# An encoder layer in a list-scheduled kernel: later copies, another DRAM layout, fixed engines for low parts, longer score runs, and a list that may hold an engine back

## The chip, the cores and the metric

The kernel runs on one NeuronCore of a Trainium2 chip. The metric is the device time of one execution in microseconds; the kernel before is given as the median of three runs. One further execution was taken with the hardware profiler.

## The reference

One encoder layer with shared weights is applied to two batches: a prompt of 512 tokens and a sample of 1024 tokens, both 1024 wide.

```python
h = rmsnorm(x, norm_g)
proj = h @ w_in
qa, ka, va, za, qb, kb, vb, zb, ga, gb = jnp.split(proj, ...)
qa = rmsnorm(qa..., qn_a)
ka = rmsnorm(ka..., kn_a)
oa = neighbourhood_attention(qa, ka, va, rpb_a) * jax.nn.silu(za)
oa = oa @ w_o_a
qb = rmsnorm(qb..., qn_b)
kb = rmsnorm(kb..., kn_b)
ob = window_gqa_attention(qb, kb, vb, t5_table, sink_b) * jax.nn.silu(zb)
ob = ob @ w_o_b
merged = jax.nn.sigmoid(ga) * oa + jax.nn.sigmoid(gb) * ob
return x + merged @ w_out
```

Branch A has 8 heads of 64; each query sees a clamped window of 8 rows by 16 columns on a grid 64 wide, with a bias per head (`rpb_a`). Branch B has 8 query heads on 2 key heads, a band of 128 tokens to either side, a T5 bias and a sink logit.

## The kernel before

Products are made in fp32r with both factors split into a high and a low part, three matmuls for each product: high by high, low by high, high by low. For activations the parts are `hh` and `hl`, for weights `whi` and `wlo`. A low part is one subtraction, source less high part.

The program has four stages one after the other: attention of the prompt (0 to about 220 us), its dense part (to about 394), attention of the sample (394 to about 787), its dense part (to the end). TensorE takes products of a next stage as filler (written to PSUM tag `d`) while it works on attention.

**Attention** goes through six groups: four of branch A (two heads each) and two of branch B (four heads each). A group's weights are loaded and split (L603, L605, L610), its token tiles are projected (L764, tag `p`), squared and summed (`sq` L783, `ss` L788), GpSimd makes the inverse norm (`rs_v` L795, `rs_r` L802), VectorE scales (`qk` L819), TensorE transposes (L864) into `kt` and `q`. Scores are products of 64-row halves of the array, two heads at once (L937), reduced with the bias and the maximum by VectorE (L972), exponentiated, transposed (L1029), weighed with v (L1066), and the tile `ot` is stored to DRAM `o_d` (L1090 for A, L1102 for B). The bias tables of a group are made from a mask and a loaded `raw` by L698. Branch B's projection reads copies `hb` of `hh` and `hl` in another token order (L665 on ScalarE, L667 on VectorE).

**The dense part** loads `ot` back (L1535, in `post_z`), multiplies by the SiLU of the product with z's weights, and stores `u_d` (L1520). Products in this part are of Strassen's form: their moving side are sums `T` of token blocks, stored beforehand in DRAM (`t_d`), loaded by L1245 and split into high and low in `split` (high on ScalarE L1172, low on VectorE or GpSimd L1177); the weights' sums `S` are split in the same way. The matmuls are at L1293 to L1295.

**What sets the order.** Every operation is entered in a class `Flow` with a list of (engine, time in ns) choices, its inputs, and a priority (smaller is more urgent). `Flow.run` plays the program through with these times: each engine that is free takes the most urgent ready operation that has room for its results; between two engines it takes the one that would be done first. Two-input operations of VectorE and GpSimd are kept apart in this plan. The order found becomes the fixed order of each engine's instructions; DMAs are issued in order by SP. On the chip each engine waits in this order for its semaphores. PSUM has banks of tag `p` (2), `x` (5, scores, transposes and sums share them) and `d` (1).

The steps of the prediction touch `project`, `attend`, `weigh`, `split`, `stored_sums`, `weight_tiles`, `post_z` and `Flow.run`.

Of the kernel before, what the change touches and what calls it, by code (L numbers as in the profile page):

```python
# [26 lines left out]
SLACK = 1.1  # L27
SCRATCH = 1024
# [12 lines left out]
P = 128  # L41
# [95 lines left out]
class Op:  # L137
    __slots__ = ("choice", "emit", "new", "vals", "after", "outs", "prio", "left", "lag", "key", "eng", "port")


class Flow:
# [20 lines left out]
    def op(self, choice, emit, prio, new=(), use=(), into=(), after=(), hold=(), lag=0, port=None):  # L162
# [6 lines left out]
        o.key, o.outs, o.eng = len(self.ops), [], None  # L169
# [37 lines left out]
    def run(self):  # L207
        import heapq

        for o in self.ops:  # L210
            o.left = len(o.after)
            for a in o.after:
                a.outs.append(o)
# [45 lines left out]

        def backlog(e, item):  # L260
            return max(free_at[e], now) + sum(dict(x.choice)[e] for p, k, x in ready[e] if (p, k) < item[:2] and x.eng is None)
# [5 lines left out]
        while done < len(self.ops):  # L267
            for e in ready:
                while free_at[e] <= now:
                    skipped, got = [], None  # L270
                    while ready[e]:
                        item = heapq.heappop(ready[e])
                        o = item[2]
                        if o.eng is not None:
                            continue
                        ns = dict(o.choice)[e]
                        if all(room(v, n) for v, n in o.new) and not any(locked(v, e) or v.held and not v.t for v in o.vals) and not barred(o, e) and all(
                            e2 == e or backlog(e2, item) + n2 >= now + ns - BIAS.get((e, e2), 0) for e2, n2 in o.choice
                        ):
# [18 lines left out]
                    if got.lag:  # L298
                        dma_free = max(dma_free, now + ns + 650) + got.lag
                        at(dma_free + 950, 2, got)  # L300
            if not events:
# [53 lines left out]
def encoder_kernel(  # L355
# [48 lines left out]
    o_d = {geo.nt: dpool.tile([2, 8, P, geo.nt], F32, tag=f"o_d{geo.nt}", name=f"o_d{geo.nt}") for geo in (gp, gs)}  # L404
# [246 lines left out]
    def attention_phase(geo, hh, hl, h_ops, mask_d, early, late):  # L651
# [79 lines left out]
        def project(br, w, t, prio):  # L731
# [10 lines left out]
            else:  # L742
# [6 lines left out]
                for q in range(2):  # L749
                    for m, v in enumerate((hh, hl)):  # L750
# [5 lines left out]
                            prio - 1, new=[hb[m][q]], hold=[v], after=[o for u in h_ops.values() for o in u], port=True,  # L756
# [154 lines left out]
        def attend(br, gi, g, batch, nb_t, info, prio):  # L911

            nh = 2 if br == "A" else 4
            k0 = 2 * (gi % 2)
            states = []
            for block in batch:
                sums = tuple(tile_([P, 4], F32, tag, 3) for tag in ("mx", "sm", "rs", "es"))
                pss = [bank("x") for _ in range(nh)]
# [7 lines left out]
            def emit(e):  # L926

                for block, _, pss, _ in states:
                    runs, tiles, width, step, whole = places(block)
                    q = queries(block)  # L930
                    for pair in range(nh // 2):
                        at = runs[0][0] if whole else pair * P
                        for n, (u, k) in enumerate(((0, 0), (0, 1), (1, 0))):
                            for i in range(2):
                                rows = slice(64 * i, 64 * i + 64)
                                kv = kt.t[rows, k0 + k].rearrange("p (t n) -> p t n", n=P)
                                pe.matmul(  # L937
                                    pss[2 * pair + i].t[:, :width], q.t[rows, u, at : at + P],
# [3 lines left out]
            def queries(block):  # L942
# [5 lines left out]
                (("pe", ns),), emit, prio, new=[v for _, _, pss, sbs in states for v in (*pss, *sbs)],  # L948
# [12 lines left out]
        def weigh(br, gi, g, block, sums, pss, sbs, nb_t, info, prio):  # L961
# [7 lines left out]
            def score(i, ps, sb):  # L969
                def emit(e, i=i, ps=ps, sb=sb):  # L970
                    init = 3.0e38 if br == "A" else nsink[:, 4 * g + i : 4 * g + i + 1]
                    dve.tensor_tensor_reduce(  # L972
                        out=sb.t[:, :width], in0=ps.t[:, :width], in1=bias_of(br, nb_t, i, table), scale=1.0,
# [18 lines left out]
            for i, (ps, sb) in enumerate(zip(pss, sbs)):  # L992
                score(i, ps, sb)
# [57 lines left out]
            for i in range(2):  # L1051
                for c in range(nw):
# [16 lines left out]
                    o = f.op((("pe", PE_(256 if br == "A" else 512)),), emit, prio, use=[v, pp], **kw)  # L1069
            ot = tile_([P, 4, P], F32, "ot_", 2)  # L1070
# [5 lines left out]
            if br == "A":  # L1076
# [10 lines left out]
                def emit():  # L1087
                    if len(runs) == 1:
                        dst = over(o_d[nt][0, g], runs).rearrange("(i p) n -> p i n", i=2)
                        nc.sync.dma_start(dst, ot.t[:64, ::2])  # L1090
                        return
                    for i in range(2):
                        dst = over(o_d[nt][0, g, 64 * i : 64 * i + 64], runs)
# [3 lines left out]
            else:  # L1097
                for e in range(2):
                    dst = o_d[nt][e, 4 + 2 * g : 6 + 2 * g, :, runs[0][0] : runs[0][0] + P]
                    dst = dst.rearrange("c (i d) n -> d (c i) n", d=64)  # L1100
                    o = sp(
                        lambda e=e, dst=dst: nc.sync.dma_start(dst, ot.t[e * 64 : e * 64 + 64]),  # L1102
                        131072, prio, use=[ot],
                    )
                    for c in (4 + 2 * g, 5 + 2 * g):
                        for n in range(nt // 512):
                            stores[c, n].append(o)
# [3 lines left out]
        for gi, (br, g) in enumerate(groups):  # L1111
# [14 lines left out]
            for t in range(nb):  # L1126
# [4 lines left out]
                size = 2 if br == "A" else 1  # L1131
# [7 lines left out]
    def dense_phase(geo, hh, hl, h_ops, o_stores, exps_done, start, opened, tp, up, p0, p1, p2, x_t, y_t, classic, fill, after_gates=None, side=None):  # L1139
# [28 lines left out]
        def split(hi, lo, src, n, prio, new_hi, new_lo, src_v, after=()):  # L1168
# [7 lines left out]
                any_tt(n),  # L1176
# [59 lines left out]
        def stored_sums(prio, d, after):  # L1236

            tv, ops = {}, {}
            for j in (1, 2, 0, 3):
                tv[j] = tuple(f.value(tp, [P, 4, nh], F32R, "T", 8) for _ in range(2))  # L1240
                vh, vl = tv[j]
                for k in range(4):
# [7 lines left out]
                        (vh, k == 0), (vl, k == 0), [st],  # L1250
# [9 lines left out]
        def weight_tiles(operands, per, prio):  # L1260
# [5 lines left out]
            for i, src in enumerate(operands):  # L1266
                at, q = [], 0
                while q < 4:
# [7 lines left out]
                        (hi, ti not in seen), (lo, ti not in seen), [src],  # L1276
# [72 lines left out]
        def pair_strassen(srcs, post, prio, mov_h, mov_t, seed=None, last=False, kept=None):  # L1349
# [11 lines left out]
            w = weight_tiles([*first, s2, s3, s1, raw[1, 1], s4], 6, prio - 0.5)  # L1361
# [162 lines left out]
        def post_z(c, a, n, v, in_psum, prio):  # L1524
# [3 lines left out]
            for e, ot in enumerate(ots):  # L1528
                if c < 4:
                    src, dst = o_d[nt][e, c, :, a : a + n], lambda ot=ot: ot.t[:, :n]  # L1530
                else:
                    src = o_d[nt][e, c].rearrange("p (i n) -> p i n", n=P)[:, :, a // nb : a // nb + m]
                    dst = lambda ot=ot: ot.t[:, :n].rearrange("p (i n) -> p i n", n=m)
                dma(
                    lambda dst=dst, src=src: nc.sync.dma_start(dst(), src), 512 * n, prio - 0.5, new=[ot],  # L1535
# [418 lines left out]
```

## Time and profile before

| | |
|---|---|
| median of 3 runs | 1136.02 us (1134.59 to 1136.24) |
| profiled execution | 1135.29 us, of it 1133.5 us span |
| granted TensorE clock | 1.00 |
| DMA issued by the kernel | 184.91 MB in 139010 packets |

The profile lists for each engine its busy time in the span and its share. A table by windows gives busy time by stretch. In a row of a timeline stand start, duration, engine, line, operation, output and input, count; in square brackets the idle time of the engine just before it and what ended that. The chain of waits is followed back from the last instruction. PE is TensorE, DVE VectorE, ACT ScalarE, POOL GpSimd, SPq the queue of SyncE.

### The profile page before, as it was taken

The page shows a single profiled execution, that of the slowest core. Times are in us where ns is not written, and L with a number is a line of the kernel's source. Part 1 is how long each engine was busy: PE and PEld are TensorE (multiplying, and loading weights), DVE is VectorE, ACT ScalarE, POOL GpSimd, SP SyncE. Part 2 cuts the span into 40 slices and gives each one's busy share as a digit, 9 for nine tenths or more (in the row PEclk, how much of TensorE's full clock was granted, in tenths as well). Part 3 has the DMA queues.
Part 4 walks back from the last instruction along what each step waited for, and adds up shares of the span by engine and source line. Part 5 has one row for each costly group of instructions (what it writes and reads, how often), then busy time and mean ns, then how long its engine had stood idle before and what let it go on. Part 6 is the DMA issues. An engine that isn't in the chain of part 4 may idle for free.

```text
span 1133.5 us, 18690 instructions
## 1 busy us (share of the span) xinstructions
PE 1119.0 (99%) x6079; PEld 973.2 (86%) x6079; DVE 860.1 (76%) x1988; ACT 651.9 (58%) x1499; POOL 337.3 (30%) x438
## 2 busy tenths in 40 slices
PE   8999999999999999999999999999999999999998
PEld 6999988888888889999999988988788888888887
DVE  5888797587776568787878888885988766677764
ACT  6777987644432257565769888876543335423430
POOL 4653433000011154434324344420333322222211
PEclk9999999999999999999999999999999999999999
DMA  7854543488886732121212314244977645867862
GB/s 263 276 155 138 184 115 103 110 257 248 256 278 216 254 128 91 27 63 30 82 41 85 81 38 112 57 131 121 307 241 234 224 156 170 281 207 222 280 215 93
DMA packets 139108, 186.11 MB, mean 164 GB/s; under 512 B 29897, under 2 KB 68561, under 8 KB 139010
## 3 DMA queue, kind: packets, MB, share of 16 engines
q1 hardware_dynamic: 139010, 184.91, 51.8%
q8 instruction: 48, 0.79, 0.3%
q14 instruction: 50, 0.41, 0.1%
HBM read 137.66 MB, written 51.92 MB: 167 GB/s over the span
## 4 chain that ended last, share of the span: by engine, by line
PE 93%; DMA 2%; DVE 2%; issue 1%; ACT 1%; POOL 1%; SPq 0%; DVEq 0%; ACTq 0%
PE p L764 25%; PE x L1294 9%; PE x L1295 9%; PE x L1293 9%; PE x L1066 5%; PE x L937 5%; PE x L1029 5%; PE d L1293 4%; PE d L1295 4%; PE d L1294 4%; PE p L1294 4%; PE p L1295 4%; PE p L1293 4%; PE x L864 2%; DMA w<-in_w_att_dram 1%
## 5 line engine op out<-in xcount | busy, mean ns | idle before, releaser
L764 PE MATMUL p<-whi,hh 128*128 128x384 f32 x384 | 133.4, 348 | 0.0
L764 PE MATMUL p<-whi,hl 128*128 128x384 f32 x384 | 132.2, 344 | 0.0
L764 PE MATMUL p<-wlo,hh 128*128 128x384 f32 x384 | 131.8, 343 | 0.0
L1172 ACT ACTIVATE whi<-raw 128x512 fp32r<-128x512 f32 (+1 forms) x140 | 81.4, 600 | 71.2 <-PE x L1294 22.3
L981 ACT ACTIVATE sb<-sb,mx 128x384 f32<-128x384 f32 (+1 forms) x192 | 107.8, 565 | 16.9 <-DVE mx L972 16.5
L1295 PE MATMUL x<-T,wlo 128*128 128x512 f32 x280 | 108.9, 389 | 0.0
L1294 PE MATMUL x<-T,whi 128*128 128x512 f32 x280 | 108.9, 389 | 0.0
L1293 PE MATMUL x<-T,whi 128*128 128x512 f32 x280 | 108.9, 389 | 0.0
L764 PE MATMUL p<-whi,hb 128*128 128x384 f32 x384 | 107.6, 346 | 0.0
L1177 POOL TENSOR_TENSOR wlo<-raw,whi 128x512 fp32r<-128x512 f32 (+1 forms) x33 | 39.5, 1204 | 215.6 <-DMA raw<-in_w_g_dram 112.9
L1040 DVE TENSOR_TENSOR pp<-x,pp 128x512 fp32r<-128x512 f32 (+1 forms) x136 | 82.5, 638 | 19.6 <-ACT pp L1035 19.0
L1177 DVE TENSOR_TENSOR wlo<-raw,whi 128x512 fp32r<-128x512 f32 (+1 forms) x107 | 72.0, 682 | 32.3 <-ACT whi L1172 28.7
L802 POOL TENSOR_TENSOR rs_r<-rs_v,mhalf 128x4 f32<-128x4 f32 (+1 forms) x72 | 80.5, 1118 | 5.7
L1035 ACT ACTIVATE pp<-x 128x512 fp32r<-128x512 f32 (+1 forms) x136 | 70.8, 559 | 15.8 <-PE x L1029 14.3
L1294 PE MATMUL x<-hl,whi 128*128 128x512 f32 x200 | 77.8, 389 | 0.0
L1295 PE MATMUL x<-hh,wlo 128*128 128x512 f32 x200 | 77.8, 389 | 0.0
L1293 PE MATMUL x<-hh,whi 128*128 128x512 f32 x200 | 77.8, 389 | 0.0
L1066 PE MATMUL x<-pp,v 128*128 128x256 f32 (+1 forms) x368 | 75.8, 322 | 0.0
L764 PEld LDWEIGHTS p<-whi,hl 128*128 128x128 f32 x384 | 72.6, 189 | 1.3 <-issue 1.0
L764 PEld LDWEIGHTS p<-wlo,hh 128*128 128x128 f32 x384 | 72.7, 189 | 1.0 <-issue 0.7
L764 PEld LDWEIGHTS p<-whi,hh 128*128 128x128 f32 x384 | 72.7, 189 | 0.7 <-DVE v L812 0.3
L764 PEld LDWEIGHTS p<-whi,hb 128*128 128x128 f32 x384 | 69.1, 188 | 3.1 <-issue 1.3
(388 smaller groups left out, 2965.1 us busy)
## 6 DMA issues: line engine op xcount, KB each, us to landing
raw<-in_w_g_dram SPq DMA_DIRECT2D x84, 256.0 KB
w<-in_w_att_dram SPq DMA_DIRECT2D x46, 384.0 KB
raw<-in_w_z_dram SPq DMA_DIRECT2D x40, 256.0 KB
ot<-o_d SPq DMA_DIRECT2D x36, 256.0 KB
g_d<-C SPq DMA_DIRECT2D x34, 256.0 KB
fr<-in_w_g_dram SPq DMA_DIRECT2D x28, 256.0 KB
raw<-in_w_out_dram SPq DMA_DIRECT2D x28, 256.0 KB
out_dram<-C SPq DMA_DIRECT2D x19, 256.0 KB
```

The lines of the kernel that those rows point to most:

```text
L764: pe.matmul(ps.t[:, :GW], part[u](k), mv.t[:, c], start=k == 0 and m == 0, stop=k == KC - 1 and m == 2,)
L802: lambda e: nc.gpsimd.tensor_tensor(r.t[:, :nn], rv.t[:, :nn], mhalf[:, :nn], op=ALU.pow),
L937: pe.matmul(pss[2 * pair + i].t[:, :width], q.t[rows, u, at : at + P], kv[:, tiles[0] : tiles[-1] + 1 : step], start=n == 0, stop=n == 2,)
L981: act.activation(sb.t[:, :width], sb.t[:, :width], AF.Exp, bias=mx.t[:, i : i + 1], scale=-1.0, accum_out=sm.t[:, i : i + 1],)
L1035: lambda e, pt=pt, pp=pp, nn=nn: act.activation(pp.t[:, 0, :nn], pt.t[:, :nn], AF.Copy),
L1040: lambda e, pt=pt, pp=pp, nn=nn: dve.tensor_tensor(pp.t[:, 1, :nn], pt.t[:, :nn], pp.t[:, 0, :nn].bitcast(F32), op=ALU.subtract),
L1066: pe.matmul(out(), v.t[:, vs], mv(), start=first, stop=last)
L1172: (("act", ACT_(n)),), lambda e: act.activation(hi(), src(), AF.Copy), prio,
L1177: lambda e: engines[e].tensor_tensor(lo(), src(), hi().bitcast(F32), op=ALU.subtract), prio,
L1293: pe.matmul(out, hi.t[:, cs], mh(), start=first and k == 0, stop=False, **more)
L1294: pe.matmul(out, hi.t[:, cs], ml(), start=False, stop=False, **more)
L1295: pe.matmul(out, lo.t[:, cs], mh(), start=False, stop=last and k == len(ws) - 1, **more)
```

## The change

There are five parts.

1. The copies `hb` wait, beside the normalised input, for the start of a step that lies six priorities ahead of them.
2. Branch B's attention output has a DRAM tensor of its own, `ob_d`, with 512 tokens in a row. A block of the prompt is stored in one DMA (128x4x128), a block of the sample in two (128x4x64, pieces of 256 bytes; before 64x4x128 in two, pieces of 512 bytes). Loads of it read whole rows of 2 KB; before, those of the sample read 8x64 (pieces of 256 bytes).
3. The low parts of the stored sums `T` from `t_d`, and of the weights of the first Strassen pair, go to VectorE alone.
4. The prompt's branch A scores of four blocks are one run of 24 matmuls instead of two runs of 12, and two blocks share a PSUM bank, in halves of 256 columns. The third and later kept z products wait for the last weighted sum of attention.
5. In attention, the list passes over an operation of ScalarE, VectorE or GpSimd if one that is more urgent by over 3 becomes ready within half of its duration.

The diff, cut to its core (line numbers of the kernel after are some 27 to 31 higher than before):

```diff
+PATIENT = ("act", "dve", "pool")
+URGENT = 3
+SHARE = 0.5
+DENSE_TOO = 0
+AHEAD = 6
...
+        def expect(o, end):
+            for x in o.outs:
+                x.open -= 1
+                x.eta = max(x.eta, end + min(self.LAG.get((o.eng, e), 100) for e, _ in x.choice))
+                if not x.open and x.eta > now:
+                    coming[x.choice[0][0]].append(x)
+
+        def sooner(o, e, ns):
+
+            if e not in PATIENT or o.slack == 1 and not DENSE_TOO:
+                return False
+            coming[e] = [x for x in coming[e] if x.eta > now and x.eng is None]
+            t = [x.eta for x in coming[e] if x.prio < o.prio - URGENT and x.eta < now + SHARE * ns]
+            if t:
+                at(min(t), 4, None)
+            return bool(t)
...
-... and not barred(o, e) and all(
+... and not barred(o, e) and not sooner(o, e, ns) and all(
...
-    o_d = {geo.nt: dpool.tile([2, 8, P, geo.nt], F32, ...) for geo in (gp, gs)}
+    o_d = {geo.nt: dpool.tile([4, P, geo.nt], F32, ...) for geo in (gp, gs)}
+    ob_d = {geo.nt: dpool.tile([geo.nt // 512, 8, P, 512], F32, ...) for geo in (gp, gs)}
...
-                            prio - 1, new=[hb[m][q]], hold=[v], after=[o for u in h_ops.values() for o in u], port=True,
+                            prio - 1, new=[hb[m][q]], hold=[v], port=True,
+                            after=[*(o for u in h_ops.values() for o in u), f.begun[nt, prio - AHEAD]],
...
+            shared = br == "A" and nt == NT_P
...
-                pss = [bank("x") for _ in range(nh)]
+                second = shared and len(states) % 2
+                pss = [(v, 256) for v, _ in states[-1][2]] if second else [(bank("x"), 0) for _ in range(nh)]
...
+            f.weighed = o
...
-                for e in range(2):
-                    dst = o_d[nt][e, 4 + 2 * g : 6 + 2 * g, :, runs[0][0] : runs[0][0] + P]
...
+                m, t = 512 // nb, runs[0][0] // P
+                for n in range(nt // 512):
+                    dst = ob_d[nt][n, 4 * g : 4 * g + 4, :, t * m : t * m + m].rearrange("a p m -> p a m")
...
-                size = 2 if br == "A" else 1
+                size = 1 if br == "B" else 4 if nt == NT_P else 2
...
-        def split(hi, lo, src, n, prio, new_hi, new_lo, src_v, after=()):
+        def split(hi, lo, src, n, prio, new_hi, new_lo, src_v, after=(), both=True):
...
-                any_tt(n),
+                any_tt(n)[: 1 + both],
...
-                        (vh, k == 0), (vl, k == 0), [st],
+                        (vh, k == 0), (vl, k == 0), [st], both=d is m_d,
...
-            w = weight_tiles([*first, s2, s3, s1, raw[1, 1], s4], 6, prio - 0.5)
+            w = weight_tiles([*first, s2, s3, s1, raw[1, 1], s4], 6, prio - 0.5, prio > 0)
...
-                    src = o_d[nt][e, c].rearrange("p (i n) -> p i n", n=P)[:, :, a // nb : a // nb + m]
+                    src = ob_d[nt][a // nh, 2 * c - 8 : 2 * c - 6, e * 64 : e * 64 + 64, :n]
...
-            o = product(ps, ws[0], mov_h(0, 0), i / 4 - 1, True, True)
+            o = product(ps, ws[0], mov_h(0, 0), i / 4 - 1, True, True, [f.weighed] if i > 1 else [])
```

TensorE issues the same matmuls before and after; VectorE has 26 rows of its order fewer and GpSimd 17 more, most of it bias tables and softmax scalings (`sb`) that change engines. The order of all engines is the same from about 825 us on. Three places show how the order moves.

The first is the start of the sample's attention, VectorE. `w_` with a number is a weight buffer of group 0 or 1. Before:

```order
L1177 TENSOR_TENSOR fl<-fr,fh 128x512
L610 TENSOR_TENSOR wlo<-w_4898,whi 128x768
L788 TENSOR_REDUCE ss<-sq 128x4
L812 TENSOR_TENSOR v<-p,v 128x2x64
L667 CAST hb<-hl 128x512 x2
L788 TENSOR_REDUCE ss<-sq 128x4
L819 TENSOR_TENSOR qk<-p,rs_r 128x256
```

After:

```order
L1207 TENSOR_TENSOR fl<-fr,fh 128x512 x2
L816 TENSOR_REDUCE ss<-sq 128x4
L840 TENSOR_TENSOR v<-p,v 128x2x64
L847 TENSOR_TENSOR qk<-p,rs_r 128x256
L637 TENSOR_TENSOR wlo<-w_4883,whi 128x768
```

The first `qk` follows its `ss` and `v` directly; the copies are gone from there, and a weight's low part comes behind. On GpSimd, before:

```order
L1166 TENSOR_TENSOR raw<-raw 128x512 x4
L1177 TENSOR_TENSOR fl<-fr,fh 128x512
L795 TENSOR_SCALAR rs_v<-ss 128x4
L802 TENSOR_TENSOR rs_r<-rs_v,mhalf 128x4
L795 TENSOR_SCALAR rs_v<-ss 128x4
```

After:

```order
L1196 TENSOR_TENSOR raw<-raw 128x512 x3
L823 TENSOR_SCALAR rs_v<-ss 128x4
L830 TENSOR_TENSOR rs_r<-rs_v,mhalf 128x4
L637 TENSOR_TENSOR wlo<-w_4891,whi 128x768
L725 TENSOR_TENSOR bias<-mask,raw 128x24x8
```

The first `rs_v` no longer stands behind a low part `fl`. On SP, where the loads for this place are issued, before:

```order
L1329 DMA s_d<-raw 128x512
L603 DMA w_4838<-in_w_att_dram 128x768
L1329 DMA s_d<-raw 128x512
L603 DMA w_4852<-in_w_att_dram 128x768
L1583 DMA out_dram<-C 128x512
L1329 DMA s_d<-raw 128x512 x2
L603 DMA w_4882<-in_w_att_dram 128x768
```

After:

```order
L1359 DMA s_d<-raw 128x512 x4
L1612 DMA out_dram<-C 128x512
L630 DMA w_4838<-in_w_att_dram 128x768
L630 DMA w_4846<-in_w_att_dram 128x768
L1633 DMA fr<-in_w_g_dram 128x512 x2
L1612 DMA out_dram<-C 128x512
L630 DMA w_4883<-in_w_att_dram 128x768
```

Group 0's weights move behind all of the `s_d` stores.

The second place is the second group of the sample's attention, VectorE, where its bias tables are made. Before:

```order
L812 TENSOR_TENSOR v<-p,v 128x2x64
L1083 TENSOR_TENSOR ot__5863<-ot__5863 64x2x128
L698 TENSOR_TENSOR bias<-mask,raw 128x24x8 x2
L698 TENSOR_TENSOR bias<-mask,raw 128x16x8 x2
L819 TENSOR_TENSOR qk<-p,rs_r 128x256
```

After:

```order
L1115 TENSOR_TENSOR ot__5801<-ot__5801 64x2x128
L847 TENSOR_TENSOR qk<-p,rs_r 128x256
L725 TENSOR_TENSOR bias<-mask,raw 128x24x8
L816 TENSOR_REDUCE ss<-sq 128x4
L725 TENSOR_TENSOR bias<-mask,raw 128x16x8
```

Two of the four table instructions leave VectorE there, and the other two stand behind a `qk` instead of ahead of it.

The third is the sample's z products, VectorE (`T` low parts, `S` sums, `C` and `ot` of the z gates). Before:

```order
L1177 TENSOR_TENSOR wlo<-S,whi 128x256
L1166 TENSOR_TENSOR U<-fr,x 128x512
L1177 TENSOR_TENSOR T<-U,T 128x512
L1166 TENSOR_TENSOR ot<-ot 128x512
L1177 TENSOR_TENSOR T<-w_10666,T 128x512
L1166 TENSOR_TENSOR C<-C,ot 128x512
L1166 TENSOR_TENSOR U<-U,x 128x512
```

After:

```order
L1207 TENSOR_TENSOR T<-fh,T 128x512
L1207 TENSOR_TENSOR T<-U,T 128x512
L1207 TENSOR_TENSOR T<-w_10643,T 128x512
L1207 TENSOR_TENSOR T<-U,T 128x512
L1196 TENSOR_TENSOR U<-U,x 128x512
L1196 TENSOR_TENSOR ot<-ot 128x512
```

The third set's `T` from `w_` stands ahead of the second `ot`, where it stood behind it.

More of the change, by code (lines that the diff above doesn't have):

```diff
@@ L137 @@
 class Op:
-    __slots__ = ("choice", "emit", "new", "vals", "after", "outs", "prio", "left", "lag", "key", "eng", "port")
+    __slots__ = ("choice", "emit", "new", "vals", "after", "outs", "prio", "left", "lag", "key", "eng", "port", "slack", "open", "eta")
 class Flow:
@@ L210, in run @@
         for o in self.ops:
-            o.left = len(o.after)
+            o.left = o.open = len(o.after)
+            o.eta = 0
             for a in o.after:
@@ L276, in run @@
                         ns = dict(o.choice)[e]
-                        if all(room(v, n) for v, n in o.new) and not any(locked(v, e) or v.held and not v.t for v in o.vals) and not barred(o, e) and all(
+                        if all(room(v, n) for v, n in o.new) and not any(locked(v, e) or v.held and not v.t for v in o.vals) and not barred(o, e) and not sooner(o, e, ns) and all(
                             e2 == e or backlog(e2, item) + n2 >= now + ns - BIAS.get((e, e2), 0) for e2, n2 in o.choice
@@ L403, in encoder_kernel @@
     t_d = dpool.tile([4, 4, P, NT_S // 2], F32, tag="t_d", name="t_d")
-    o_d = {geo.nt: dpool.tile([2, 8, P, geo.nt], F32, tag=f"o_d{geo.nt}", name=f"o_d{geo.nt}") for geo in (gp, gs)}
+    o_d = {geo.nt: dpool.tile([4, P, geo.nt], F32, tag=f"o_d{geo.nt}", name=f"o_d{geo.nt}") for geo in (gp, gs)}
+    ob_d = {geo.nt: dpool.tile([geo.nt // 512, 8, P, 512], F32, tag=f"ob_d{geo.nt}", name=f"ob_d{geo.nt}") for geo in (gp, gs)}
     s_d = dpool.tile([4, 4, P, 512], F32, tag="s_d", name="s_d")
@@ L947, in attend @@
             o = f.op(
-                (("pe", ns),), emit, prio, new=[v for _, _, pss, sbs in states for v in (*pss, *sbs)],
+                (("pe", ns),), emit, prio, new=[v for _, _, pss, sbs in states for v in (*(ps for ps, a in pss if not a), *sbs)],
                 use=[queries(block) for block in batch], after=[o for b in batch for t in b[1] for o in info[t][2]],
@@ L990, in score @@
                 x.vals = [*x.vals, mx]
-            for i, (ps, sb) in enumerate(zip(pss, sbs)):
-                score(i, ps, sb)
+            for i, ((ps, a), sb) in enumerate(zip(pss, sbs)):
+                score(i, ps, a, sb)
             if br == "B":
@@ L1088, in emit @@
                     if len(runs) == 1:
-                        dst = over(o_d[nt][0, g], runs).rearrange("(i p) n -> p i n", i=2)
+                        dst = over(o_d[nt][g], runs).rearrange("(i p) n -> p i n", i=2)
                         nc.sync.dma_start(dst, ot.t[:64, ::2])
@@ L1092, in emit @@
                     for i in range(2):
-                        dst = over(o_d[nt][0, g, 64 * i : 64 * i + 64], runs)
+                        dst = over(o_d[nt][g, 64 * i : 64 * i + 64], runs)
                         nc.sync.dma_start(dst, ot.t[:64, 2 * i].rearrange("p (a b) -> p a b", b=64))
```

29 lines of the change are left out of this document (14 added, 15 removed).

## The prediction

> **What bounds the kernel now.** I read the busy times first, then TensorE by stretches, then the waits of TensorE.
>
> ```profile
> span 1133.5 us, 18690 instructions
> PE 1119.0 (99%) x6079; PEld 973.2 (86%) x6079; DVE 860.1 (76%) x1988; ACT 651.9 (58%) x1499; POOL 337.3 (30%) x438
> ...
> 0.00:50.00 50.00, 44.03 (x249) 39.14 (x250) 34.90 (x94) 33.99 (x72) 24.23 (x40) 1.00 0.80 278
> 50.00:100.00 50.00, 50.00 (x325) 46.92 (x324) 40.29 (x129) 36.51 (x97) 29.49 (x48) 1.00 0.56 175
> ...
> 400.00:450.00 50.00, 48.16 (x308) 44.98 (x308) 38.57 (x114) 31.12 (x80) 24.63 (x34) 1.00 0.34 108
> 450.00:500.00 50.00, 49.24 (x334) 46.59 (x331) 40.94 (x119) 29.12 (x81) 18.24 (x29) 1.00 0.17 46
> 650.00:700.00 50.00, 49.77 (x317) 44.20 (x316) 44.14 (x121) 43.46 (x109) 20.05 (x30) 1.00 0.30 80
> ...
> 800.00:850.00 50.00, 47.52 (x206) 38.07 (x205) 46.19 (x67) 22.98 (x46) 18.43 (x13) 1.00 0.83 268
> ```
>
> The columns are the stretch, its length, then busy time of TensorE, weight loads, VectorE, ScalarE and GpSimd, the granted clock and the DMA share. TensorE works 99% of the span at a clock of 1.00, with 6079 matmuls that the change leaves as they are. So no change of copies or layouts can win much: what can be won is the holes in TensorE's row, and there are few. They lie at the start (5.97 us up to 50) and in the four other stretches below 50.00.
>
> ```profile
> PE x L1811 <- DMA rb<-in_norm_row_dram: 4.4, 1, 4.4
> PE x L864 <- DVE qk L819: 3.1, 3, 1.8
> PE d L1294 <- DVE T L1177: 1.6, 1, 1.6
> ...
> PE p L1294 <- DVE T L1177: 0.9, 2, 0.7
> ```
>
> Of the start, 4.4 is the first load, which the change does not touch. The rest are transposes that wait for a normalised q/k tile, and low-part products that wait for a low part T made by VectorE. I go through these places in turn, and measure a hole as the distance between two starts less the distance without a wait.
>
> **Place A, start of the sample's attention.**
>
> ```profile
> 403.98 0.40 PE L1294 MATMUL d<-hl,fh 128*128 128x512 f32 x1
> 404.21 0.40 PE L1295 MATMUL d<-hh,fl 128*128 128x512 f32 x1
> 406.45 0.44 PE L864 MATMUL x<-ident,qk 128*128 128x128 f32 x2 [1.84 <-DVE qk L819]
> ...
> 402.62 2.15 DVE L667 CAST hb<-hl 128x512 fp32r<-128x512 f32 x2
> 405.97 0.42 DVE L819 TENSOR_TENSOR qk<-p,rs_r 128x256 f32<-128x256 f32 x1 [0.75 <-POOL rs_r L802]
> ...
> 402.23 1.31 POOL L1177 TENSOR_TENSOR fl<-fr,fh 128x512 fp32r<-128x512 f32 x1 [11.40 <-ACT fh L1172]
> 403.62 1.22 POOL L795 TENSOR_SCALAR rs_v<-ss 128x4 f32<-128x4 f32 x1
> 404.92 1.01 POOL L802 TENSOR_TENSOR rs_r<-rs_v,mhalf 128x4 f32<-128x4 f32 x1
> ```
>
> Starts lie 2.24 apart; such a product takes 0.23 (404.21 less 403.98), so the hole is 2.0, some 0.17 more than the marked wait. The awaited qk needs rs_r, which GpSimd began late behind fl (1.31). The two casts of hb (2.15) sit on the same engine as qk and feed branch B, which comes some 200 us later. The change ties those copies to the start of a step near them, and in the new order fl is no longer ahead of rs_v, and VectorE takes qk before the next weight's low part. I take the whole 2.0 as gone. What is late next is the weights:
>
> ```profile
> 396.26 3.98 DMA w<-in_w_att_dram
> ```
>
> SP issued group 0's first two weights between the s_d stores; now all four s_d stores and an output store go ahead of the first weight, and two fr loads ahead of the third. A load of them took 3.98 to land (a row of the chain), so a shift of 2 to 3 us in the queue arrives as such, and the TensorE work between covers part of it. I put a new hole at 0.9, between 0 and 2.0 (the old one again). Net for A: −1.1, from −2.0 to 0.
>
> **Place B.**
>
> ```profile
> 465.02 1.57 DVE L698 TENSOR_TENSOR bias<-mask,raw 128x192 f32<-128x192 f32 x4 [0.65 <-DMA raw<-rpb_x]
> 466.52 0.41 DVE L819 TENSOR_TENSOR qk<-p,rs_r 128x256 f32<-128x256 f32 x1
> ...
> 465.97 0.34 PE L764 MATMUL p<-wlo,hh 128*128 128x384 f32 x1
> 467.08 0.30 PE L864 MATMUL x<-ident,qk 128*128 128x128 f32 x1 [0.76 <-DVE qk L819]
> ```
>
> Four bias tables waited 0.65 for a DMA, and qk stood behind them in VectorE's order: the hole is 1.11 − 0.17 = 0.94. After, GpSimd takes 16 of VectorE's bias instructions over the whole kernel, and the raw load is issued earlier; VectorE keeps two tables here. −0.8, from −0.94 to 0. The 0.23 missing between 650 and 700 I halve, with its start-to-start loss near 0.5 as the upper end: −0.3.
>
> **Place D, the sample's z products.**
>
> ```profile
> 785.75 1.24 SPq L1102 DMA_DIRECT2D o_d<-ot__10494  x2
> ...
> 791.71 2.14 SPq L1535 DMA_DIRECT2D ot<-o_d  x2
> ...
> L1520 SPq DMA_DIRECT2D u_d<-C x10: 319/428/3656, 791.3 to 838.1; - x10
> ...
> 803.77 6.24 DMA ot<-o_d
> ...
> 803.26 0.68 DVE L1177 TENSOR_TENSOR T<-U,T 128x512 fp32r<-128x512 f32 x1
> 810.10 1.25 DVE L1166 TENSOR_TENSOR ot<-ot 128x512 f32<-128x512 f32 x1 [0.46 <-DMA ot<-o_d]
> 811.27 1.75 DVE L1177 TENSOR_TENSOR T<-w,T 128x512 fp32r<-128x512 f32 x1
> ...
> 810.76 1.71 POOL L1177 TENSOR_TENSOR wlo<-raw,whi 128x512 fp32r<-128x512 f32 x1
> ...
> 811.11 0.40 PE L1293 MATMUL d<-T,whi 128*128 128x512 f32 x1
> 813.08 0.50 PE L1294 MATMUL d<-T,whi 128*128 128x512 f32 x1 [1.57 <-DVE T L1177]
> ...
> 818.37 0.50 PE L1294 MATMUL p<-T,whi 128*128 128x512 f32 x1 [0.24 <-DVE T L1177]
> ...
> 820.67 0.50 PE L1294 MATMUL p<-T,whi 128*128 128x512 f32 x1 [0.65 <-DVE T L1177]
> ```
>
> Two causes add up. The loads of ot from o_d come in 256-byte pieces: their issues take SP 2.14 for two, and the u_d store behind them took up to 3.66 to issue where the median of its line is 0.43, so t_d loads that stand behind go out some 3 us late, and ot itself landed after 6.24 (a row of the chain). VectorE waited for ot with T<-w behind it in order. And T took 1.75 beside a GpSimd instruction of 1.71, where the same T takes 0.68 alone. The holes: 1.97 − 0.23 = 1.74 at 813.08, again 0.17 above the marked wait; 0.24 and 0.65 become 0.41 and 0.82 in the same way, together 2.97. I allow 0.5 more for small ones around. The change makes branch B's loads contiguous 2 KB rows, issues the t_d loads ahead of them, keeps T on VectorE alone and lists it ahead of ot; GpSimd has no T in that stretch. VectorE carries one more T (0.68), in a stretch where it is 46.19 of 50 busy. −2.9, from −3.4 to 0.
>
> On the 256-byte pieces the change also does the reverse: 32 stores of the sample's branch B go from 512-byte to 256-byte pieces (the prompt's stay at 512). They lie in the sample's attention, where the DMA share was 0.17 and 0.30 in the stretches shown, and the first load from there was issued 4.7 us after the last store (791.71, and 785.75 with 1.24 of issue). I price them at 0; without that cover a store as slow as the 6.24 above would hold the first ot back by about 1.5 (6.24 − 4.7). The Trainium skill (DMA: Bandwidth & Descriptors, Specifications) says that transfers under 512 B fall to read-modify-write and miss the line rate; the trace's slow 256-byte loads agree, and by that rule these stores would be slower too, which is the third rival below.
>
> **Score runs.** Four prompt blocks now share one run, so four runs of TensorE's row-split mode fewer.
>
> ```profile
> 38.20 0.33 PE L764 MATMUL p<-wlo,hh 128*128 128x384 f32 x1
> 38.46 0.97 PE L937 MATMUL x<-kt,qt 64*128 64x256 f32 x12
> 39.37 0.44 PE L864 MATMUL x<-ident,qk 128*128 128x128 f32 x2
> ```
>
> Entering took 0.26 instead of 0.17, and the twelve took 0.91, where six pairs of 256 columns at half of 0.23 would be 0.69: 0.3 a run, four times 0.3 is −1.2, from −1.2 to 0. Against it: a run holds its four score banks of five until eight score reductions are done, not four. VectorE, 40.29 of 50 busy there, has room, and TensorE has projection and filler work to go on with, so I take no hole from it beyond the general one below. The prompt's hb copies leave the first stretch, whose holes beside the first load are 5.97 − 4.4 = 1.6, and its first tiles are moved: a quarter of that, −0.4, from −1.0 to +0.7. The z products that now wait for the last weighted sum of attention cost 0, since projection and filler products stand between.
>
> **New holes.** The list is new from the start to 220 us and from 394 to 825; the dense part after 825 keeps its order. Old holes in this part: 2.0 + 0.94 + 0.5 + 3.47 = 6.9. They come from what the planner does not see, DMA landings and the shared slowness of VectorE and GpSimd, so a new list draws new ones. It is some 650 us of order by the same planner, and its transfers and engines are as little known to it as before. I take less than a third of the old sum, because half of them (the z holes) had a cause that the change takes away, and the rule that holds an engine back for an urgent operation works against the other kind. +2.0, from 0 to 6.9.
>
> **The sum.** −1.1 − 0.8 − 0.3 − 2.9 − 1.2 − 0.4 + 2.0 = −4.7. The profiled execution took 1135.29 (its span and 1.8 around it), so 1130.6; the median of the three runs shown stands 0.73 above it, so 1131.3.
>
> **The rivals.** First, all goes and nothing new comes: −6.7 with no 0.9 and no 2.0 is −7.6, 1128.4. For it speaks the rest of the span, where the order stays and TensorE is full; against it every earlier draw of this planner left holes. Second, new holes as many as the old: −6.7 + 6.9 is 0, 1136.2, no change. For it speaks that place B hangs on one late DMA, which no planner's rule here sees. Third, the change doesn't do what it says for transfers: the stores in 256-byte pieces make the first ot late and half of D's gain is lost, −4.7 + 1.5 + 1.5 = −1.7, 1134.3. Fourth, slower: at the z products GpSimd's low parts of weights and sums meet VectorE's T. Each meeting adds 1.75 − 0.68 = 1.07 to a full VectorE, and TensorE waits for it. The row at 811.27 is one. D's 2.9 lost makes 1134.2, and four meetings more make 1138.5, slower than before. From two further meetings upward it is at the old time. Against it speaks that GpSimd's two low parts and one T between 807 and 812 no longer lie beside T in the order. The Trainium skill (Trainium Architecture — The Big Picture, What this means for kernel authors) calls the port pair of the two engines an exclusive lock, not a split. The rows agree, 1.75 beside 1.71; by that rule a meeting could cost the whole 1.71, and two or three would do.
>
> **How the numbers follow.** Forecast 0.55 (1131.3, its own range 1129.0 to 1133.7); all gone 0.16 (1128.4); as many new holes 0.15 (1136.2); slow pieces 0.06 (1134.3); port meetings 0.08 (1138.5). A measurement of this kernel tells no less than about 0.2%, 2.3 us. Under 1133.7 lie the first two and a little of the others: faster 0.73 (0.55 × 0.9 + 0.16 and 0.07 of the rest). Within 2.3: most of the second rival and the third, 0.18. Slower, the fourth and a little of the second: 0.09. The range goes from 1127.5 to 1136.4: below lies half of the first rival's lower side, above the fourth and a part of the second.
>
> **What would show it.** Right: no wait of L864 for qk at 404; no wait for T between 808 and 821, ot landing within 3 us, u_d issues at 0.42; stretch 800:850 at 49.5 or more; four runs of 24 in the prompt. Wrong: waits of TensorE for whi or wlo of group 0 near 400 of over 1; new rows of waits between 50 and 200 above 2 us together; T at 1.75 again.

## The result, and the profile after

The changed kernel takes 1225.54 us (1225.13 to 1225.87) against 1135.3 us before: a ratio of 1.0798, 95% interval 1.0781 to 1.0815. It is slower by 90 us. The prediction was 1131.3 us, with 1127.5 to 1136.4 as its range: the measured time lies far above it.

The page of the changed kernel, its span, the busy times and the granted clock in 40 slices:

```profile
span 1223.8 us, 18684 instructions
...
PE 1148.1 (94%) x6079; PEld 987.8 (81%) x6079; DVE 855.0 (70%) x1951; ACT 655.5 (54%) x1503; POOL 359.8 (29%) x471
...
PEclk9999999997999999999999999998897799999999
```

TensorE issues its 6079 matmuls as before but is busy for 1148.1 us instead of 1119.0. The span is 90.3 longer: 29.1 of this is longer busy time, and 61.2 is idle time (75.7 instead of 14.5). The clock row shows where the matmuls were slow. The windows, with the columns as in the prediction:

```profile
250.00:275.00 25.00, 17.08 (x74) 13.46 (x73) 8.90 (x17) 3.31 (x6) 0.00 (x0) 0.94 0.28 90
275.00:300.00 25.00, 14.66 (x48) 11.17 (x48) 7.38 (x11) 5.70 (x9) 0.00 (x0) 0.77 0.43 135
...
850.00:875.00 25.00, 20.06 (x62) 14.03 (x63) 19.34 (x25) 9.23 (x20) 10.72 (x9) 0.75 0.55 175
...
925.00:950.00 25.00, 12.35 (x33) 9.03 (x34) 10.21 (x16) 6.07 (x11) 2.71 (x3) 0.66 0.26 90
950.00:975.00 25.00, 11.30 (x35) 8.42 (x34) 10.82 (x16) 4.10 (x8) 2.18 (x2) 0.73 0.39 133
```

The loss lies in both dense parts. In these stretches the other engines have idle time too: VectorE is busy for 7 to 11 of 25 us in four of the five (19.34 in the fifth), ScalarE for 3 to 9, and the DMA engines for a quarter to a half. The clock falls to 0.66 where TensorE has long gaps, and its matmuls there take longer: the same `x<-T,whi` matmul has a median of 628 ns between 925 and 975, where the shortest takes 390 ns. The Trainium skill (TensorE: Matmul & The Clock Gate, HAM oscillation) describes that: gaps above some 3.4 us throttle the array, and the work after them runs at half clock. The trace agrees in kind, 0.66 to 0.94 as means over these stretches, with gaps of up to 8.8 us (next view).

TensorE's waits:

```profile
PE x L1325 <- DVE wlo L1207: 26.4, 4, 7.6
PE x L1323 <- ACT whi L1202: 17.2, 2, 8.8
PE p L1325 <- DVE wlo L1207: 6.8, 3, 5.3
...
PE x L892 <- DVE qk L847: 1.0, 3, 0.4
```

The wait for qk has become smaller, from 3.1 to 1.0. What is new are waits for split weights. The engines that split them were themselves waiting. VectorE's idle time ahead of instructions on `ot`, in the changed kernel:

```profile
L1564 SPq DMA_DIRECT2D ot<-ob_d x24: 474/507/743, 244.8 to 956.1; - x24
...
  DMA ot<-ob_d: 99.2, 12
```

12 waits, 99.2 us, so 8.3 us each. SP's queue and VectorE at the first of them:

```profile
244.84 1.72 SPq L1564 DMA_DIRECT2D ot<-ob_d  x2
247.24 12.60 SPq L1287 DMA_DIRECT2D raw<-in_w_g_dram  x2
259.90 1.10 SPq L1564 DMA_DIRECT2D ot<-ob_d  x2
```

```profile
258.19 0.69 DVE L1196 TENSOR_TENSOR ot<-ot 128x512 f32<-128x512 f32 x1 [8.98 <-DMA ot<-ob_d]
```

Two loads of 256 KB, issued from 244.84 on, were there at 258.19. The row of 12.60 behind them joins two loads of weights. The first took 2.64 to issue; the second was issued at 259.51, after SP had waited 9.6 for a weight's low part `wlo` on VectorE, and VectorE stood still for `ot`. So one late load holds up VectorE, what stands behind `ot` in its order, and the loads that wait for VectorE. The next `ot` shows how this reaches TensorE:

```profile
272.71 0.69 DVE L1196 TENSOR_TENSOR ot<-ot 128x512 f32<-128x512 f32 x1 [7.90 <-DMA ot<-ob_d]
274.88 0.69 DVE L1207 TENSOR_TENSOR wlo<-raw,whi 128x512 fp32r<-128x512 f32 x1
275.62 0.79 PE L1325 MATMUL x<-hh,wlo 128*128 128x512 f32 x1 [7.60 <-DVE wlo L1207]
```

The transfers in the first stretch (248 to 257), busy share and GB/s in 40 slices:

```profile
DMA  1011101111194897111110111101111101111011
GB/s 36 27 36 55 55 36 55 55 55 55 55 164 109 273 410 300 55 55 55 55 55 36 55 55 55 55 36 55 55 55 55 55 36 55 55 55 55 36 55 55
```

The bandwidth is about 55 GB/s in most slices, and mostly under two tenths of the 16 DMA engines are busy. In between, another load reaches 410. So the loads from ob_d run on a few engines only. The trace's records of single packets say how many: packets of 2 KB take 84 ns in the median, and for 7.1 of the 9 us exactly two packets are under way at once. Their source is written as 2 x 64 x 512 (two heads, 64 rows of each), and the two heads don't lie next to each other: the outermost dimension counts 2. The old loads were written as 128 rows, in the sample each of 8 x 64. 512 KB at 55 GB/s is 9.5 us, near the wait of 8.98.

The Trainium skill has the rule (DMA: Bandwidth & Descriptors, Why a DMA increments its semaphore by 16 and not by 1): a transfer is spread over the largest number of engines up to 16 that divides the slowest dimension, not of size 1, of both sides. With 2 that is two engines; the trace agrees, with two packets at a time. I weighed another section of that page, on pieces under 512 bytes, and not this one.

### The profile page after: what moved, and what is told of

Its sections match the earlier page's. It is cut to its first block, busy times and chain, and to the rows that moved or that the text cites. A ratio compares the mean times of both kernels' runs of the same rounds, so it can differ in the third digit from the quotient of the medians.

```text
span 1223.8 us, 18684 instructions
## 1 busy us (share of the span) xinstructions
PE 1148.1 (94%) x6079; PEld 987.8 (81%) x6079; DVE 855.0 (70%) x1951; ACT 655.5 (54%) x1503; POOL 359.8 (29%) x471
## 4 chain that ended last, share of the span: by engine, by line
PE 56%; DMA 7%; issue 2%; DVE 2%; SPq 1%; ACT 1%; POOL 0%; DVEq 0%; ACTq 0%; POOLq 0%
PE p L792 17%; DMA ot<-ob_d 5%; PE x L1324 5%; PE x L1323 5%; PE x L1325 5%; PE x L1097 3%; PE x L1060 3%; PE x L968 3%; PE p L1324 2%; PE d L1323 2%; PE p L1325 2%; PE p L1323 2%; PE d L1325 2%; PE d L1324 2%; PE x L892 1%
## 5 line engine op out<-in xcount | busy, mean ns | idle before, releaser
L1323 PE MATMUL x<-T,whi 128*128 128x512 f32 x280 | 113.2, 404 | 21.0 <-ACT whi L1202 17.2
L1325 PE MATMUL x<-T,wlo 128*128 128x512 f32 x280 | 112.6, 402 | 5.7 <-DVE wlo L1207 5.5
L1324 PE MATMUL x<-T,whi 128*128 128x512 f32 x280 | 112.9, 403 | 1.2 <-DVE T L1207 1.1
L1325 PE MATMUL x<-hh,wlo 128*128 128x512 f32 x200 | 81.5, 408 | 20.9 <-DVE wlo L1207 20.9
L1323 PE MATMUL x<-hh,whi 128*128 128x512 f32 x200 | 80.7, 404 | 2.5 <-ACT hh L1202 2.5
L830 POOL TENSOR_TENSOR rs_r<-rs_v,mhalf 128x4 f32<-128x4 f32 (+1 forms) x72 | 81.2, 1128 | 5.8
L1323 PEld LDWEIGHTS x<-T,whi 128*128 128x128 f32 x280 | 54.6, 195 | 34.0 <-ACT whi L1202 18.0
L1324 PE MATMUL x<-hl,whi 128*128 128x512 f32 x200 | 80.7, 403 | 0.2 <-DVE hl L1207 0.2
L1196 DVE TENSOR_TENSOR ot<-ot 128x512 f32<-128x512 f32 x12 | 8.3, 692 | 99.2 <-DMA ot<-ob_d 99.2
L1207 POOL TENSOR_TENSOR wlo<-raw,whi 128x512 fp32r<-128x512 f32 (+1 forms) x35 | 42.4, 1218 | 111.5 <-ACT whi L1202 111.5
```

The costliest lines, as they stand in the source:

```text
L830: lambda e: nc.gpsimd.tensor_tensor(r.t[:, :nn], rv.t[:, :nn], mhalf[:, :nn], op=ALU.pow),
L1207: lambda e: engines[e].tensor_tensor(lo(), src(), hi().bitcast(F32), op=ALU.subtract), prio,
L1323: pe.matmul(out, hi.t[:, cs], mh(), start=first and k == 0, stop=False, **more)
L1324: pe.matmul(out, hi.t[:, cs], ml(), start=False, stop=False, **more)
L1325: pe.matmul(out, lo.t[:, cs], mh(), start=False, stop=last and k == len(ws) - 1, **more)
```

## The experiments

**The loads.** All are timed beside the kernel before; the ratio is to it.

*Two halves.* Each load from ob_d is issued as two, one for each head:

```diff
+                    for i in range(2):
+                        nc.sync.dma_start(ot.t[64 * i : 64 * i + 64, :n], src[i])
```

> The changed kernel, but each load of ot from ob_d is issued as two loads of 64x512 (one per head) instead of one whose source is 2 x 64 x 512. Theory 1 (a transfer whose outermost dimension counts 2 runs on only two of the 16 DMA engines; nothing else is wrong): the loss goes, about 1131 us, between 1128 and 1135; the loads land within 4 us. Theory 2 (the place or pitch of ob_d in DRAM, or its 256-byte stores, make it slow): still about 1225 us. Theory 3 (the new order of the list makes the waits): still above 1200 us.

1140.63 us, ratio 1.0051 (1.0037 to 1.0065). The loss of 90 us goes; the order of every engine is the same as in the changed kernel, and the same bytes from the same place are now nearly hidden. VectorE's wait for them in this kernel, and in the kernel before its waits for all loads of `ot`:

```profile
  DMA ot<-ob_d: 6.4, 7
```

```profile
DVE ot L1166 <- DMA ot<-o_d: 7.7, 7, 2.3
...
DVE C L1166 <- DMA ot<-o_d: 6.6, 3, 6.2
```

Theories 2 and 3 fall as causes of the 90 us. But the kernel is 6 us slower than before, not 4.7 faster, and outside the 1128 to 1135 that theory 1 gave: it was right on the cause and wrong on what is left.

*The layout alone*, put into the kernel before (part 2 only):

> The kernel before with only the new DRAM layout of branch B's output (part 2). Theories 1 and 2: about as slow as the changed kernel, 1215 to 1235 us. Theory 3: about 1136 us, the loads hidden as before.

1226.79 us, 1.0811 (1.0797 to 1.0825). The layout alone makes the whole loss.

*The old layout*, with all other parts of the change:

> The changed kernel with the old DRAM layout (all parts but part 2). Theories 1 and 2: 1129 to 1135 us, the forecast sum without what the layout was to give at the z products, so about 1132. Theory 3: above 1200 us.

1139.6 us, 1.004 (1.0027 to 1.0053). No loss of 90, and again no gain: the forecast of 1129 to 1135 was missed.

*Branch A's loads with an outermost 2*, in the kernel before, by a block padded to 65 rows:

```diff
+    oa_d = {geo.nt: dpool.tile([4, 2, 65, geo.nt], F32, ...) for geo in (gp, gs)}
...
+                    src, dst = oa_d[nt][c, :, :64, a : a + n], lambda ot=ot: ot.t[:, :n]
```

> The kernel before, where only branch A's output gets a tensor with a padded row block (4 x 2 x 65 x tokens), so that its 12 loads have a source of 2 x 64 x 512; stores, sizes, pitch and order stay. Theory 1: each of these loads moves at about 50 GB/s and takes 5 us or more, the kernel is 20 to 50 us slower, 1156 to 1186 us. Theories 2 and 3: no change, 1134 to 1138 us.

1174.71 us, 1.0352 (1.0333 to 1.0371), 40 us slower, inside the forecast range. SP's queue, the waits for these loads (on VectorE, one of them on GpSimd), and the rate between 226 and 234 in this kernel:

```profile
224.55 1.11 SPq L1536 DMA_DIRECT2D ot<-oa_d  x2
225.77 5.13 SPq L1258 DMA_DIRECT2D raw<-in_w_z_dram  x1
230.94 6.00 SPq L559 DMA_DIRECT2D xt<-in_xt_s_dram  x2
```

```profile
  DMA ot<-oa_d: 60.5, 12
```

```profile
GB/s 138 123 141 166 41 8 18 15 15 23 23 38 8 28 51 51 51 51 51 51 51 51 51 51 51 51 51 113 133 133 225 369 366 338 294 284 340 317 325 317
```

51 GB/s again, two packets at a time, in a tensor that the change never touched, with pieces of 2 KB as ob_d's. The number of the outermost dimension is enough. The issues behind take 5.13 and 6.00; in the kernel before the same two rows are

```profile
226.34 0.37 SPq L1257 DMA_DIRECT2D raw<-in_w_z_dram  x1
226.76 2.92 SPq L558 DMA_DIRECT2D xt<-in_xt_s_dram  x2
```

**Parts undone, from the changed kernel with the loads in two halves.**

*Part 3 undone:*

```diff
-                any_tt(n)[: 1 + both],
+                any_tt(n),
```

> The changed kernel with the loads in two halves, and part 3 undone (low parts may go to GpSimd everywhere). TensorE's order is the same as with part 3. Theory: in that kernel TensorE lost 4.6 us to T between 809 and 822, since VectorE carries all of T while GpSimd makes low parts beside it (T at 1.69 and 1.77 us instead of 0.68); undone, some T go to GpSimd and VectorE has room: 1 to 3 us faster than with the halves alone. Rival: loads of t_d come late because of their queue, not VectorE: no change, within 1 us.

1136.67 us, 1.001 (0.9995 to 1.0025), by the ratios 0.4% less than with it: the theory's direction held, and the gain is more than its 1 to 3 us. The profiled executions don't show the gain (1139.67 us, and 1138.93 with part 3), though TensorE's wait for T in them falls from 3.5 to 2.3.

*Part 4's runs undone* (two blocks a run, no shared banks):

> The changed kernel with the loads in two halves, and the score runs of part 4 undone (two blocks a run, no shared banks). Theory: the runs of four win 1.9 us of TensorE service but hold four of five banks, and the new holes of 3.4 us between 57 and 190 come with them: undone 1 to 2 us faster than with the halves alone. Rival: the holes come from the list's waiting rule: then undone is about 2 us slower.

1141.16 us, 1.0052 (1.0036 to 1.0068), no change. The theory's mechanism is seen: between 50 and 200 TensorE is busy for 150.00 of 150 us, with the runs 147.43. But the gain of 1 to 2 us did not show in the time; the profiled execution loses 3.4 between 340 and 400 instead (see the table).

*Part 5 switched off:*

```diff
-SHARE = 0.5
+SHARE = 0
```

> The changed kernel with the loads in two halves, and the list's waiting rule of part 5 switched off. Theory: the rule took away the holes at the start of the sample's attention and of its second group (2.0 and 0.9 us), so switched off it is about 3 us slower; the holes of the prompt stay. Rival: the rule makes the holes in the prompt: then about 3 us faster, with no hole between 57 and 190.

1141.4 us, 1.005 (1.0033 to 1.0066), no change either. At the start of the sample's attention the hole comes back, and GpSimd shows why:

```profile
402.57 1.29 POOL L1207 TENSOR_TENSOR fl<-fr,fh 128x512 fp32r<-128x512 f32 x1 [11.28 <-ACT fh L1202]
403.95 0.19 POOL L823 TENSOR_SCALAR rs_v<-ss 128x4 f32<-128x4 f32 x1
404.23 1.01 POOL L830 TENSOR_TENSOR rs_r<-rs_v,mhalf 128x4 f32<-128x4 f32 x1
```

fl stands ahead of rs_v again. The prompt's holes mostly close (148.97 of 150), as the rival said. What the one gave, the other took.

*Part 1 undone:*

```diff
-                            after=[*(o for u in h_ops.values() for o in u), f.begun[nt, prio - AHEAD]],
+                            after=[o for u in h_ops.values() for o in u],
```

> The changed kernel with the loads in two halves, and part 1 undone (copies as early as buffers allow). Theory: the copies come back to the start of the sample's attention and the hole of 2.0 us there with them: 1 to 3 us slower. Rival: the hole there was fl on GpSimd and not the copies: no change, within 1 us.

1137.98 us, 1.002 (1.0007 to 1.0032). Both views were wrong in the sum: it became faster, by 0.3%. The hole at the sample's start did not come back (see the table), as the rival said: copies early don't make it.

**The layout on its own, and two combinations.**

*The layout in two halves, in the kernel before:*

> The kernel before with only the new layout of branch B's output, its loads issued in two halves of 64x512. Theory: with all 16 engines at work the layout itself costs nothing; of the 3.4 us lost at the z products part goes, since ot lands sooner: 1 to 3 us faster than before. Rival: what TensorE waits for there is T on VectorE, slowed by GpSimd, and not the loads: within 1 us of before.

1139.96 us, 1.0035 (1.0022 to 1.0049). At the z products the mechanism was right, the waits of TensorE for T there are small in this kernel:

```profile
PE x L865 <- DVE qk L820: 3.3, 5, 1.2
PE x L1292 <- ACT hh L1171: 2.9, 1, 2.9
PE x L1030 <- DVE sb L1014: 1.6, 1, 1.6
...
PE d L1293 <- DVE T L1176: 0.5, 1, 0.5
...
PE p L1293 <- DVE T L1176: 0.2, 1, 0.2
```

0.7 us for T, before 2.5. Yet waits of 2.9 for hh and 1.6 for sb are new, in an order that hardly moved. The forecast of a gain failed.

*One load of 128x512* (the dimensions of ob_d in another order, stores of 64 rows):

```diff
+    ob_d = {geo.nt: dpool.tile([geo.nt // 512, 2, 4, P, 512], F32, ...) for geo in (gp, gs)}
...
+                    src = ob_d[nt][a // nh, e, c - 4, :, :n]
```

> The kernel before with another order of the dimensions of branch B's tensor, so that a load is one contiguous 128x512 and a store two of 64x4x64 or 64x4x128: no transfer has an outermost dimension under 64. Theory: as the two halves, 0 to 2 us faster than those, because the loads stand in SP's queue at the stage that waits for them while the stores stand where nobody waits. Rival: small 256-byte stores delay: 1 us or more slower than the halves.

1137.56 us, 1.0022 (1.001 to 1.0035). It lies 2.4 us under the halves, but the intervals overlap: unclear.

*Parts 1 and 3 undone together:*

> The changed kernel with the loads in halves and parts 1 and 3 undone together: what stays is layout, score runs and the waiting rule. Theory: undone alone the two parts gave about 4 and 2.6 us against the halves; together 1133 to 1136 us, no slower than the kernel before. Rival: each single list is a throw of its own, and gains do not add: 1137 to 1141 us.

1136.84 us, 1.0017 (1.0004 to 1.0029), above the theory's range and just under the rival's. The two gains of undoing did not add up: undone together they give no more than part 3 alone.

*Part 5 alone, in the kernel before:*

> The kernel before with the waiting rule of part 5 alone. Theory: it removes the two holes for qk in the sample's attention (2.0 and 0.9 us): 1 to 3 us faster than before, if it makes no new ones. Rival: it re-orders all of attention and makes new holes in their place: within 1 us of before or slower.

1135.31 us, 1.0003 (0.9992 to 1.0014): no change, as the rival said.

**The other parts alone, in the kernel before, and the rest together.**

*Part 4 alone:*

> The kernel before with part 4 alone (score runs of four blocks, shared banks, later z products). Theory: TensorE's service falls by 1.9 us; if the holes between 57 and 190 belong to the runs (they went when the runs were undone), they come here too and about 1 to 2 us slower comes out. Rival: the holes need the waiting rule as well: about 2 us faster than before.

1137.72 us, 1.0028 (1.0015 to 1.0041), slower by more than the 1 to 2 us of the theory. The holes come with the runs, without the rule too (147.35 of 150 busy between 50 and 200).

*Part 1 alone:*

> The kernel before with part 1 alone (copies of hb later). Theory: undone, it gave 2.6 us; alone it costs 1 to 3 us. Rival: it takes the casts from the start of the sample's attention and the hole of 2.0 us goes: 1 to 2 us faster.

1138.02 us, 1.0031 (1.0012 to 1.005): slower as the theory said, by a little more than its 1 to 3 us.

*Part 3 alone:*

> The kernel before with part 3 alone (T's low parts on VectorE only); TensorE's order hardly moves. Theory: as undone it gave 4 us, alone it costs 2 to 4 us, by waits for T between 805 and 825. Rival: with the loads of the old layout it is the loads that are late: no change within 1 us.

1138.32 us, 1.003 (1.0016 to 1.0043): the size is the theory's, its mechanism is not seen. TensorE's waits for T are 2.7 us in the profiled execution, before 2.5; new is a wait of 1.4 for a weight's high part near 385.

*Parts 1, 4 and 5, without 2 and 3:*

> The changed kernel without parts 2 and 3 (old layout, low parts on either engine): copies, score runs and the rule. Theory: all parts but 2 were 1.0040 of before, and part 3 undone gave 4 us with the halves: about 1135 to 1136, no change. Rival: the lists do not add: 1138 to 1141.

1137.31 us, 1.0024 (1.001 to 1.0038), between theory and rival.

TensorE's busy time in four stretches of the profiled execution of each kernel, from the table by windows (the stretch's length in the head):

| kernel | rule of part 5 | 50:200 (150) | 340:400 (60) | 400:420 (20) | 800:830 (30) |
|---|---|---|---|---|---|
| before | no | 150.00 | 60.00 | 18.16 | 27.52 |
| loads in halves, all parts | yes | 147.43 | 58.93 | 19.93 | 26.38 |
| the same without part 3 | yes | 147.01 | 59.56 | 19.76 | 27.75 |
| the same without part 4's runs | yes | 150.00 | 56.59 | 19.95 | 26.46 |
| the same without part 5 | no | 148.97 | 59.80 | 18.39 | 26.46 |
| the same without part 1 | yes | 148.63 | 57.02 | 19.92 | 28.88 |
| layout in halves alone | no | 148.17 | 56.22 | 17.54 | 29.27 |
| part 5 alone | yes | 149.57 | 57.36 | 19.68 | 29.96 |
| part 4 alone | no | 147.35 | 58.83 | 18.40 | 27.88 |
| part 1 alone | no | 149.16 | 57.54 | 18.43 | 27.44 |
| part 3 alone | no | 150.00 | 58.60 | 18.46 | 27.19 |
| old layout, all other parts | yes | 147.39 | 58.29 | 18.96 | 26.65 |
| layout with one load alone | no | 150.00 | 58.92 | 17.39 | 28.22 |
| loads in halves, without parts 1 and 3 | yes | 148.62 | 58.17 | 19.72 | 28.26 |
| parts 1, 4 and 5 | yes | 147.22 | 60.00 | 19.95 | 28.43 |

Where the rule is on, 400:420 is full to 19.7 or more; where it is off, 17.4 to 18.5, with copies early or late. (The exception is the kernel with the old layout and the rule, 18.96: it keeps a wait of 1.0 for qk.) The stretch 340:400 has holes of 0.2 to 3.8 us in all variants but the last row, none in the profiled execution of before, though TensorE's order there is not changed by the parts in attention. One execution of each kernel was profiled, and executions of one kernel differ by more than these holes (1132.32 to 1140.33 us for all parts but 3 with the loads in halves). So a single hole of this size may belong to the execution and not to the order; that was not tested.

## Why the prediction was wrong, point by point

**The layout's loads (the term of place D, and the third rival).** The step that failed is "branch B's loads contiguous 2 KB rows", which was to bring part of the −2.9 and cost 90 us. The pieces are contiguous, but the transfer has two blocks of 64 rows, and it runs at 51 to 55 GB/s, two packets at a time. I counted the bytes of a piece and not the outermost dimension of the source; the load's line in the diff had it, a slice of two heads and 64 rows of each. This is all of the 90 us: the layout alone makes it (1.0811), other loads written in that way make 40 us, and in two halves it goes. Nothing in my rivals contained it: the third one allowed the layout a loss of 3.0 us, by its stores. Of that rival nothing is seen: with the loads in halves the stores have their pieces of 256 bytes, and VectorE waits less for `ot` than before (6.4 for ob_d and 5.6 for o_d, before 14.3). What the stores themselves take was not measured.

**Place A: right, with another cause than half of the text.** The hole of 2.0 went, and the weights' hole of 0.9 that I added did not come (19.93 of 20 busy with all parts and the loads in halves). The casts of hb were not the cause: with copies early and the rule on the hole is gone (19.92), with copies late and the rule off it is there (18.43). In that last kernel, as in the one without part 5, fl stands ahead of rs_v on GpSimd again, which the rule passes over. It is not the only way to a hole here: the kernel with the old layout has no fl there and still waits 1.0 for qk.

**Place B: right in size.** The stretch from 450 to 500 is full in the kernel with the halves (50.00 of 50, before 49.24).

**Place D's VectorE: wrong sign.** −2.9 was forecast. With the loads repaired TensorE is busy for 26.38 of 30 us between 800 and 830, before 27.52: 1.1 us worse. Its waits for T there:

```profile
PE p L1324 <- DVE T L1207: 2.7, 2, 2.1
...
PE d L1324 <- DVE T L1207: 0.8, 3, 0.4
```

That is 3.5, before 2.5. The fourth rival's mechanism is in the rows, VectorE's T beside GpSimd's low parts, in the kernel with the halves:

```profile
813.54 1.77 DVE L1207 TENSOR_TENSOR T<-U,T 128x512 fp32r<-128x512 f32 x1
```

```profile
813.45 1.31 POOL L1207 TENSOR_TENSOR wlo<-S,whi 128x512 fp32r<-128x512 f32 x1 [0.98 <-ACT whi L1202]
814.73 1.73 POOL L1207 TENSOR_TENSOR wlo<-raw,whi 128x512 fp32r<-128x512 f32 x1
```

The T took 1.77 instead of 0.68, and TensorE waited 0.64 for it. Taking T away from GpSimd did not keep GpSimd away from T. That is only a part: the longest wait, 2.1, is for a T that took 1.22 at 818.50 and stood behind an `ot`, an `S` and a `C` in VectorE's order. Part 3 alone costs 0.3%, and undone it gives 0.4%. The layout alone does help there (29.27 of 30), as the prediction said of the late loads.

**Score runs: service right, side effect missed.** Four runs fewer were to win 1.2 us. From the starts of all matmuls, each compared with the median distance of its kind in the trace of before, TensorE's own work falls by about 1.9 us with all parts. But holes of 2.6 us come between 50 and 200. I had named a cause, a run that holds four of the five banks until eight reductions are done, and priced it at 0 beyond the general term. That the holes belong to the runs is shown: they go when the runs are undone (150.00) and come with part 4 alone, and in the table all kernels with the runs lose 1.0 to 3.0 there, those without 0 to 1.8. That the banks make them is not shown: with part 4 alone TensorE's waits in that stretch are 2.6 for qk. Part 4 alone is 0.28% slower.

**New holes: the term of +2.0 was too small.** With the loads repaired the profiled execution has 1137.1 us of span, 3.6 more than before, where the terms without new holes give −6.7: 10.3 us apart. In the stretches above new holes are 2.6 (50 to 200) and 1.1 (340 to 400), and D's −2.9 became +1.1; these make 7.7 of the 10.3, and the rest is not placed. Of six versions of single parts, five are slower by 0.2 to 0.35% and one is level; what was won at places A, B and D's loads was lost again elsewhere. Leaving the loads aside, the second rival, new holes as many as the old, comes nearest and had 0.15, though its 1136.2 is below the 1140.63 as well. Two signs of being wrong that the prediction named came true: T at 1.77, and new waits of 2.6 between 50 and 200.

**What stays open.** Why the holes at 340 to 400 appear in most variants, with TensorE's order unchanged there, was not settled: the releaser is a split of `hh` or of weights on ScalarE, and before the weights' splits ScalarE itself waited for loads of `w_out`. Nor is it settled what part of the 6 us that are left belongs to the list. None of the sixteen versions is faster than the kernel before; the nearest are part 5 alone (1.0003) and all parts but 3 with the loads in halves (1.001).

## What to carry to other kernels

Of a DMA whose layout is changed, read the outermost dimension of both sides as written, not just the size of its contiguous pieces: a source of 2 x 64 rows that don't join moved at 51 GB/s, and the same rows as two transfers of 64 were nearly hidden. Such a transfer also holds up the queue behind it, and the matmul engine, idle, lost its clock (0.66 here), so a slow load costs more than its own wait. In a list-scheduled kernel near its bound, a term won at one place is a forecast for that place only; here the moved list had about as many new holes as the old one had.

## What the runs showed of the hardware that was not expected

- A transfer of 256 KB with an outermost dimension of 2 runs at 51 to 55 GB/s, with two packets under way at a time; SP's issue of the next transfer behind a pair of them took 5.13 us, where the same issue took 0.37 in the kernel before.
- 61 us of idle time on TensorE came with 29 us of longer busy time, at granted clocks of 0.66 to 0.94 in the stretches shown.
